# Softmax reciprocals through DRAM instead of through ACT and TensorE, in a hybrid RG-LRU and neighbourhood-attention layer

## The chip, the cores and the metric

One core of a Trainium2 chip runs the whole layer. The metric is the device time of one execution in microseconds; the number for a kernel is the median of its runs. Engines are called as in the profile: PE (TensorE), DVE (VectorE), ACT (ScalarE), POOL (GpSimd) and SP (SyncE, which here only issues DMAs). PEld is TensorE's loading of weights, which overlaps its matmuls.

## The reference

A sequence of 512 positions (a grid of 8 rows by 64 columns) with 1024 channels passes one layer: an RMS norm with a modulation, eight projections, a recurrent branch and a neighbourhood-attention branch, a gated merge and a final norm, all in float32. The change touches the attention branch (16 heads of 64 channels):

```
proj = h @ w_in;  xa, za, q, k, v, zb, ga, gb = split(proj)
for each grid row r:                       # its window is all 8 rows, 16 columns around the query's column
    s = einsum('bqhd,bwqkhd->bhqwk', q_r, k_win) * scale + bias
    p = softmax(s over the window)
    out_r = einsum('bhqwk,bwqkhd->bqhd', p, v_win)
y_b = out * silu(zb)
y_b = y_b @ w_pb
```

The kernel leaves the exponentials unnormalized. The product of p and v comes out with channels on the partitions and queries along the row. The sums of the softmax come out the other way: queries on the partitions, and one column for each block and head. Their reciprocals have to be brought from that layout to the other one, to every channel of the head, and are multiplied into silu(zb).

## The kernel before

The first part normalizes x and computes v (tiles hx), which goes to DRAM (vscr) and comes back in another layout (vt). Then comes a sequence of projections, each 24 matmuls of 128x128 by 512 columns into one PSUM bank (acc). Every float32 operand is split into a high part and a low part (whi and wlo, qh and ql, kh and kl, ybh and ybl), and three products replace one. ACT makes the high parts, DVE or POOL the low ones. The weights (wraw) come by DMA, 512 KB each, some projections ahead.

Attention runs over eight pairs of heads (`pr`). Each pair has three projections (q, k, z) and then `attention`: the scores (PSUM tiles sp, 24 matmuls, which read qh, ql, kh and kl), the bias and minimum on DVE (L721), exponentials on ACT with the sums into sm (L727), transposes of p (pt), the split pp, the product with vt (pv), and its three parts added up (vp, yt). While one pair is in its softmax, PE works on the projections of the next. The columns are cut into four blocks of 16 (`b`); a block's 128 queries lie on the partitions, so that sm is 128 x 8, two heads for each of four blocks. The last steps of a pair are

- rc (L775): the reciprocals of sm on DVE, 128 x 8
- rcx (L779): ACT repeats each of them 64 times, with a factor of 0.5, to 128 x 512
- rcb (L784): PE transposes the four 128x128 blocks into a PSUM bank (its tile is listed as mi)
- szr (L786): DVE multiplies sz, which is silu(zb) without its factor 0.5, by them
- yb (L788): DVE multiplies that by yt, then come ybh on ACT and ybl on DVE

ybh and ybl are read by the projections with w_pb, after all eight pairs.

The order of the instructions is made by a planner before the program is built (`Plan`). Every operation is given its engine, a cost, a rank and the tiles that it reads and writes; the planner places them one by one at the earliest estimated time. It hands out buffers of fixed pools (36 tiles of 2 KB a partition, 32 of 4 KB, 8 PSUM banks, with limits for each kind). `lock` keeps a DVE operation and one on POOL apart in that plan. The result is a fixed order on each engine, SP's queue included: an engine that waits for one operation holds back all that stands behind it. The bias (braw) is loaded by two DMAs a pair and made up on POOL (nb); vt is loaded by eight DMAs for every second pair.

Of the kernel before, what the change touches and what calls it, by code (L numbers as in the profile page):

```python
# [8 lines left out]
F32 = mybir.dt.float32  # L9
F32R = mybir.dt.float32r  # L10
AF = mybir.ActivationFunctionType
ALU = mybir.AluOpType

P = 128
# [54 lines left out]
class Plan:  # L69
# [18 lines left out]
    def op(self, eng, cost, fn, rank, r=(), w=(), rw=(), lock=False, after=(), spare=0, size=0, until=None, name=""):  # L88
        o = Op()
        o.alts = {eng: cost} if isinstance(eng, str) else dict(zip(eng, cost))  # L90
        o.fn, o.rank, o.lock, o.spare, o.size, o.name = fn, rank, lock, spare, size, name
        o.n, o.until = len(self.ops), until
        deps = set()
        for t in list(r) + list(rw):
            for f in t.family():
                deps.update(f.writers)
        for t in list(w) + list(rw):
            for f in t.family():
                deps.update(f.readers)
        for t in r:  # L100
            t.readers.append(o)
        for t in w:
            t.writers.append(o)
        for t in rw:
            for f in [t] + t.parts:
                f.writers, f.readers = [], []
            t.writers = [o]
        o.tiles = list(dict.fromkeys(t.base or t for t in list(w) + list(rw) + list(r)))
        for t in o.tiles:
            t.uses += 1  # L110
        o.data, o.succ, o.t = set(deps), [], 0.0
        deps.update(after)
        o.left = len(deps)
        for d in deps:
            d.succ.append(o)
        self.ops.append(o)
        return o
# [155 lines left out]
def act(n, ptr=0, acc=False):  # L273
    return 0.19 + 0.833e-3 * n + 0.093 * ptr + 0.19 * acc


def dve(n):
    return 0.153 + 1.043e-3 * n
# [15 lines left out]
def layer(ctx, tc, x, par, w_m, w_g, bc_gate, w_v, w_in, w_blk, rpb, amask, w_pa, w_pb, w_o, g_final, out):  # L294
    nc = tc.nc
# [4 lines left out]
    dp = ctx.enter_context(tc.tile_pool(name="dp", bufs=1, space=bass.MemoryType.DRAM))  # L300
    pl = Plan({"s": NS, "w": NW, "bank": 8}, LIMITS)
    op = pl.op
    cnt = [0]

    def nm(s):
        cnt[0] += 1
        return f"{s}_{cnt[0]}"

    def T(name, dt=F32):
        return pl.tile("s", lambda i: sb.tile([P, S], dt, tag=f"s{i}", name=nm(name)))  # L310
# [9 lines left out]
    def B(cls):  # L320
        return pl.tile(cls, lambda i: ps.tile([P, 512], F32, tag=f"b{i}", name=nm(cls)))

    def C(name, n, bufs=4):

        return pl.tile("c", lambda i: tp.tile([P, n], F32, tag=name, name=nm(name), bufs=bufs))
# [3 lines left out]
    def load(t, dst, src, rank, size, after=(), spare=0, r=(), name="load"):  # L329

        return op("SP", 0.45, lambda e: nc.sync.dma_start(dst(), src() if callable(src) else src), rank,
                  r=r, w=[t], after=after, spare=spare, size=size, name=name)
# [20 lines left out]
    def const(name, shape, dt=F32):  # L353
        return pl.fixed(cp.tile(shape, dt, name=name))

    ident, onesc, onesr = const("ident", [P, P]), const("onesc", [P, P]), const("onesr", [P, P], F32R)
# [11 lines left out]
       r=[par_sb, ident], w=[pp0])  # L368
# [54 lines left out]
    for t in range(NT):  # L423
        for h in range(2):
            a = xt[t, h] = T("x")
# [5 lines left out]
    for t in range(NT):  # L431
# [7 lines left out]
        if t % 2:  # L439
            rstd_ops(2, [qap[i], qdp[i]], lambda i=i: (qa.ap[:, 2 * i:2 * i + 2], qd.ap[:, 2 * i:2 * i + 2]), -16.8 + 2 * i, rx[i])  # L440
            for h in range(2):
                for u in (t - 1, t):
                    def scale(e, u=u, h=h, i=i):
# [6 lines left out]
                       lock=True)  # L450
# [165 lines left out]
    def proj(w, rh, rl, lo="DVE"):  # L616

        n = len(main)
        raw, hi, low = W("wraw"), W("whi", F32R), W("wlo", F32R)
        v = lambda t: (lambda: t.ap.rearrange("p (k c) -> p k c", k=KD))  # L620
        load(raw, whole(raw), w, n - 5, 524288, after=gate_of(n, 5), spare=1,
             name=f"w{n}")
        op("ACT", act(1024), cast(whole(hi), whole(raw)), n - 2.2, r=[raw], w=[hi], after=gate_of(n, 3), name=f"whi{n}")
        engs = (lo,) if isinstance(lo, str) else lo
        costs = [dve(1024) if e == "DVE" else pool_(1024) for e in engs]
        op(engs, costs, sub(whole(low), whole(raw), whole(hi)), n - 2.1, r=[raw, hi], w=[low], lock=True, name=f"wlo{n}")
        o = B("acc")
        for k in range(KD):
            def f(e, k=k):
                mm3(o.ap, v(hi)()[:, k, :], v(low)()[:, k, :], rh[k][1](), rl[k][1](), k == 0, k == KD - 1)  # L630
            first = op("PE", pe(512, 3), f, 1000 + n + 0.01 * k, r=[hi, low, rh[k][0], rl[k][0]], rw=[o], name=f"p{n}")
            if k == 0:
                main.append(first)
        return n, o


    H = (slice(0, 64), slice(64, 128))
# [3 lines left out]
    nat = lambda t: t.rearrange("p (b r c) -> p r b c", b=4, c=16)  # L641
    rbc = lambda t: t.rearrange("p (r b c) -> p r b c", b=4, c=16)
# [39 lines left out]
    def attention(pr, q, k, z, nbt, pos):  # L682
# [9 lines left out]
        sm, yt = C("sm", 8), T("yt")  # L692
# [4 lines left out]
        def scores(e_):  # L697
            for b, (kc0, w, _) in enumerate(BLOCKS):
                for i, (qt, kt) in enumerate(((qh, kh), (qh, kl), (ql, kh))):
                    for h in range(2):  # L700
                        kv = kt.ap.rearrange("p (r c) -> p r c", c=GW)[H[h], :, kc0:kc0 + w]
                        o = sps[b // 2][h].ap.rearrange("p (e f) -> p e f", e=2)[:, b % 2, :nkb[b]]
                        mm(o, qt.ap[H[h], b * P:(b + 1) * P], kv, i == 0, i == 2)
        op("PE", 1.45, scores, pos, r=[qh, ql, kh, kl], w=sps[0] + sps[1], name=f"qk{pr}")

        def half(b0):
            sp = sps[b0 // 2]
            spv = lambda h, e: sp[h].ap.rearrange("p (e f) -> p e f", e=2)[:, e, :]
            rk = pos + 0.1 * b0
            nks = nkb[b0:b0 + 2]  # L710
            pv = [B("pv"), B("pv")]
            for e in range(2):
                b, nk, w = b0 + e, nks[e], BLOCKS[b0 + e][1]
                nb = nbt[(1, 0, 0, 2)[b]]
                pt_, mn = T("p"), C("mn", 2, 16)
                hv = lambda t: t.ap.rearrange("p (h f) -> p h f", h=2)
                for h in range(2):
                    def f(e_, h=h, e=e, nk=nk, nb=nb, pt_=pt_, mn=mn):
# [49 lines left out]
        half(2)  # L768

        nz, oz = z  # L770
        sz, rc, rcb = T("sz"), C("rc", 8), B("mi")
        op("ACT", act(512), lambda e: nc.scalar.activation(sz.ap, oz.ap, AF.Tanh, scale=0.5), nz - 1.9, r=[oz], w=[sz], name="zt")
        op("DVE", dve(512), lambda e: nc.vector.scalar_tensor_tensor(sz.ap, sz.ap, 1.0, oz.ap, op0=ALU.add, op1=ALU.mult),
           nz - 1.9, r=[oz], rw=[sz], name="sz")
        op("DVE", 0.17, lambda e: nc.vector.reciprocal(rc.ap, sm.ap), pos - 0.3, r=[sm], w=[rc], name="rc")  # L775


        rx_ = T("rcx")
        op("ACT", act(512), lambda e: nc.scalar.activation(rx_.ap.rearrange("p (b c) -> p b c", b=8),  # L779
           rc.ap.unsqueeze(2).to_broadcast([P, 8, 64]), AF.Copy, scale=0.5), pos - 0.3, r=[rc], w=[rx_], name="rcx")  # L780

        def f(e_):
            for b in range(4):
                nc.tensor.transpose(rcb.ap[:, b * P:(b + 1) * P], rx_.ap[:, b * P:(b + 1) * P], ident.ap)  # L784
        op("PE", 0.47, f, pos - 0.3, r=[rx_, ident], w=[rcb], name="rcb")
        op("DVE", dve(512), lambda e: nc.vector.tensor_tensor(rbc(sz.ap), rbc(sz.ap), nat(rcb.ap), op=ALU.mult),  # L786
           pos - 0.3, r=[rcb], rw=[sz], name="szr")
        op("DVE", dve(512), lambda e: nc.vector.tensor_tensor(rbc(sz.ap), nat(yt.ap), rbc(sz.ap), op=ALU.mult), pos + 0.5, r=[yt],  # L788
           rw=[sz], lock=True, name="yb")
        ybh[pr], ybl[pr] = two("ybhl")  # L790
# [2 lines left out]
           name="ybl")  # L793
# [36 lines left out]
    for pr in range(8):  # L830
        n0 = len(main)
        nbt = bias(pr, n0, gate_of(n0, 2) if pr else [main[6]])
        if pr % 2 == 0:
            load_v(pr // 2, gate_of(n0, 2) if pr else [])
        q = proj(w_in[16 + pr], hhl, hll, LO_A if pr else "DVE")
        k = proj(w_in[24 + pr], hhl, hll, LO_A)
        z = proj(w_in[32 + pr], hhl, hll, LO_A)
        attention(pr, q, k, z, nbt, k[0] + 0.6)
# [199 lines left out]
    for k in range(KD):  # L1038
# [3 lines left out]
        for n in range(2):  # L1042
            v = lambda n=n, raw=raw: raw.ap[:, n * 512:(n + 1) * 512]
            op("DVE", dve(512), lambda e, n=n, v=v: nc.vector.tensor_tensor(v(), v(), gate[n].ap, op=ALU.mult), rank,
               r=[gate[n]], rw=[raw], lock=True, name="wog")
# [5 lines left out]
    for t in range(NT):  # L1051
        for h in range(2):
            a = xres[t, h] = T("xr")
# [51 lines left out]
    pos = [B("acc") for _ in range(NT)]  # L1105
# [8 lines left out]
    for t in range(NT):  # L1114
        for h in range(1 + (t == NT - 1)):
            w = 256 if t == NT - 1 else 512
# [87 lines left out]
```

## Time and profile before

| | before |
|---|---|
| median of 3 runs | 574.23 us (572.92 to 574.43) |
| profiled execution | 573.27 us, span 571.4 us |
| granted TensorE clock | 0.997 |
| instructions | 7735 |
| chain that ended last | PE 96%, DVE 2%, ACT 1% |
| DMA | 81.34 MB, mean 142 GB/s |

The span reaches from the first to the last instruction; the time of an execution includes a little around it. Times within the trace are given from the span's start. Attention runs from about 79 us (scores of pair 0) to about 262 us, one pair every 22.4 us. Rows of the timeline give the start, the length, the engine, the line, the operation, "output<-input" by tile names, and in brackets how long the engine sat idle and who ended it. Rows on a tile or line give the number of instructions and their shortest, median and longest duration in ns. Rows of windows give for each stretch the busy time and the number of instructions of PE, PEld, DVE, ACT and POOL, then the granted clock, the mean busy share of the 16 DMA engines and the GB/s. Matmuls overlap, so that their single durations add up to more than the time they take.

### The profile page before, as it was taken

The page shows a single profiled execution, that of the slowest core. Times are in us where ns is not written, and L with a number is a line of the kernel's source. Part 1 is how long each engine was busy: PE and PEld are TensorE (multiplying, and loading weights), DVE is VectorE, ACT ScalarE, POOL GpSimd, SP SyncE. Part 2 cuts the span into 40 slices and gives each one's busy share as a digit, 9 for nine tenths or more (in the row PEclk, how much of TensorE's full clock was granted, in tenths as well). Part 3 has the DMA queues.
Part 4 walks back from the last instruction along what each step waited for, and adds up shares of the span by engine and source line. Part 5 has one row for each costly group of instructions (what it writes and reads, how often), then busy time and mean ns, then how long its engine had stood idle before and what let it go on. Part 6 is the DMA issues. An engine that isn't in the chain of part 4 may idle for free.

```text
span 571.4 us, 7735 instructions
## 1 busy us (share of the span) xinstructions
PE 563.2 (99%) x2829; PEld 464.6 (81%) x2829; DVE 393.1 (69%) x693; ACT 336.6 (59%) x584; POOL 99.1 (17%) x84
## 2 busy tenths in 40 slices
PE   8999999999999999999999999999999999999995
PEld 6888888888888888887887787787788888888885
DVE  4997966575666657877389559749847996398323
ACT  5765537547556557478938876984894333234133
POOL 0005527374382570000000000000000000000220
PEclk9999999999999999999999999999999999999998
DMA  8993988544445322123232223123229813290002
GB/s 279 409 406 110 347 242 268 156 125 135 109 121 158 93 92 75 37 84 120 73 112 92 75 73 130 50 98 110 75 87 335 276 38 110 111 330 2 0 38 111
DMA packets 30815, 81.34 MB, mean 142 GB/s; under 512 B 3265, under 2 KB 6457, under 8 KB 30778
## 3 DMA queue, kind: packets, MB, share of 16 engines
q1 hardware_dynamic: 30633, 80.60, 42.1%
q8 instruction: 22, 0.36, 0.3%
q10 hardware_dynamic: 144, 0.26, 0.1%
q14 instruction: 16, 0.12, 0.1%
HBM read 74.56 MB, written 6.29 MB: 141 GB/s over the span
## 4 chain that ended last, share of the span: by engine, by line
PE 96%; DVE 2%; ACT 1%; issue 0%; POOL 0%; POOLq 0%; DVEq 0%; ACTq 0%
PE acc L342 77%; PE hx L342 7%; PE pv L342 3%; PE pt L736 2%; PE gt L342 2%; PE sp L342 2%; PE hx L386 1%; PE mi L784 1%; PE mi L457 1%; DVE wc L501 0%; PE hx L471 0%; ACT x L446 0%; DVE junk L436 0%; ACT xT L336 0%; ACT vh L336 0%
## 5 line engine op out<-in xcount | busy, mean ns | idle before, releaser
L342 PE MATMUL acc<-hhl,whi 128*128 128x512 f32 x784 | 246.1, 395 | 0.0
L342 PEld LDWEIGHTS acc<-hhl,whi 128*128 128x128 f32 x784 | 142.7, 188 | 29.0 <-issue 1.8
L342 PE MATMUL acc<-hhl,wlo 128*128 128x512 f32 x392 | 153.1, 390 | 0.0
L342 PEld LDWEIGHTS acc<-hhl,wlo 128*128 128x128 f32 x392 | 73.6, 188 | 16.0
L336 ACT CAST whi<-wraw 128x1024 fp32r<-128x1024 f32 x72 | 74.2, 1045 | 3.3 <-DMA wraw<-in_w_in_dram 2.5
L339 DVE TENSOR_TENSOR wlo<-wraw,whi 128x1024 fp32r<-128x1024 f32 x49 | 59.1, 1219 | 14.0 <-ACT whi L336 13.2
L339 POOL TENSOR_TENSOR wlo<-wraw,whi 128x1024 fp32r<-128x1024 f32 x23 | 56.0, 2439 | 68.4 <-ACT whi L336 47.0
L1075 POOL TENSOR_TENSOR yo<-yo,gfin 128x512 f32<-128x512 f32 x6 | 8.1, 1352 | 338.4 <-ACT xr L1072 338.3
L727 ACT ACTIVATE p<-p,mn 128x192 f32<-128x192 f32 (+1 forms) x64 | 30.4, 477 | 28.8 <-DVE mn L721 28.8
L662 POOL TENSOR_TENSOR nb<-msk,braw 128x192 f32<-128x192 f32 (+1 forms) x48 | 34.6, 756 | 55.4 <-DMA braw<-in_rpb_dram 55.4
L721 DVE CUSTOM_DVE_ANT_0 p<-sp,nb 128x192 f32<-128x192 f32 (+1 forms) x64 | 31.1, 615 | 16.7 <-PE sp L342 16.7
L342 PE MATMUL acc<-woh,mhl 128*128 128x512 f32 (+1 forms) x144 | 40.4, 365 | 0.0
L342 PE MATMUL acc<-yahl,whi 128*128 128x512 f32 x128 | 39.4, 389 | 0.0
L342 PE MATMUL acc<-ybhl,whi 128*128 128x512 f32 x128 | 39.4, 389 | 0.0
L952 DVE SCALAR_TENSOR_TENSOR gm<-gm,acc 128x512 f32<-128x512 f32 x16 | 11.0, 687 | 39.4 <-PE acc L342 39.4
L743 DVE TENSOR_TENSOR pp<-pt,pp 96x512 fp32r<-96x512 f32 (+1 forms) x32 | 22.0, 688 | 22.1 <-ACT pp L741 21.9
L342 PE MATMUL hx<-vh,hhl 128*128 128x512 f32 x112 | 35.3, 391 | 0.0
L342 PEld LDWEIGHTS acc<-woh,mhl 128*128 128x128 f32 x144 | 26.1, 189 | 4.4
L342 PEld LDWEIGHTS acc<-yahl,whi 128*128 128x128 f32 x128 | 24.0, 188 | 5.0
L342 PEld LDWEIGHTS acc<-ybhl,whi 128*128 128x128 f32 x128 | 24.0, 188 | 5.0
L342 PE MATMUL acc<-wol,mhl 128*128 128x512 f32 (+1 forms) x72 | 26.3, 365 | 0.0
L342 PE MATMUL acc<-yahl,wlo 128*128 128x512 f32 x64 | 24.9, 389 | 0.0
(186 smaller groups left out, 982.2 us busy)
## 6 DMA issues: line engine op xcount, KB each, us to landing
wraw<-in_w_in_dram SPq DMA_DIRECT2D x56, 512.0 KB
wc<-in_w_m_dram SPq DMA_DIRECT2D x16, 512.0 KB
vscr<-va SPq DMA_DIRECT2D x8, 512.0 KB
vt<-vscr SPq DMA_DIRECT2D x16, 256.0 KB
wraw<-in_w_pb_dram SPq DMA_DIRECT2D x8, 512.0 KB
wraw<-in_w_pa_dram SPq DMA_DIRECT2D x8, 512.0 KB
wr<-in_w_g_dram SPq DMA_DIRECT2D x16, 256.0 KB
wo<-in_w_o_dram SPq DMA_DIRECT2D x8, 512.0 KB
```

Source lines behind the costliest of these rows:

```text
L336: return lambda e: nc.scalar.copy(o(), i()) if e == "ACT" else nc.vector.tensor_copy(o(), i())
L339: return lambda e: ENGINE[e].tensor_tensor(o(), a(), b().bitcast(F32), op=ALU.subtract)
L342: nc.tensor.matmul(o, a, b, start=first, stop=last)
L386: op("PE", 0.9, lambda e, n=n, cb=cb: nc.tensor.matmul(cb.ap, onesc.ap[0:1, :], crow.ap[0:1, n * 512:(n + 1) * 512], start=True, stop=True ...
L457: op("PE", 0.3, lambda e: nc.tensor.matmul(wb.ap[:, :P], onesc.ap, onesc.ap, start=True, stop=True), 5000 + j, r=[onesc], w=[wb], until=un ...
L662: nc.gpsimd.tensor_tensor(o, mv, view, op=ALU.subtract)
L721: nc.vector.tensor_tensor_reduce(out=o, in0=v(spv(h, e)[:, :nk]), in1=v(hv(nb)[:, h, :nk]), scale=1.0, scalar=3e38, op0=ALU.add, op1=ALU.m ...
L727: nc.scalar.activation(hv(pt_)[:, h, :nk], hv(pt_)[:, h, :nk], AF.Exp, bias=mn.ap[:, h:h + 1], scale=-1.0, accum_out=sm.ap[:, 2 * b + h:2 ...
L736: nc.tensor.transpose(pv4()[:4 * w, h, j, :], hv(pt_)[:, h, j * 4 * w:(j + 1) * 4 * w], ident.ap)
L743: op("DVE", dve(512), lambda e_, w=w, ppv=ppv, pv4=pv4: nc.vector.tensor_tensor(ppv()[:4 * w, :, :, 1, :], pv4()[:4 * w], ppv()[:4 * w, :, ...
L952: op("DVE", dve(512), lambda e: nc.vector.scalar_tensor_tensor(t.ap, t.ap, 1.0, o.ap, op0=ALU.add, op1=ALU.mult), n - 1.9, r=[o], rw=[t], ...
L1075: op(("DVE", "POOL"), (dve(w), pool_(w)), lambda e: ENGINE[e].tensor_tensor(y(), y(), gfin[n].ap[:, gs], op=ALU.mult), rank + 0.1, r=[gfin ...
```

## The change

The reciprocals are written to a small DRAM tensor (rscr, 8 x 128, one for each pair) with their axes swapped, and read back by two DMAs, one for each head, that repeat the head's four rows of 128 queries on its 64 partitions. The factor 0.5 is put in by doubling the sums before the reciprocal. The repeat on ACT, the four transposes on PE and the PSUM bank go away; the product szr reads SBUF instead of PSUM.

```
-        sz, rc, rcb = T("sz"), C("rc", 8), B("mi")
+        sz, rc, rcx = T("sz"), C("rc", 8), T("rcx")
...
-        op("DVE", 0.17, lambda e: nc.vector.reciprocal(rc.ap, sm.ap), pos - 0.3, r=[sm], w=[rc], name="rc")
+        op("DVE", 0.34, lambda e: (nc.vector.tensor_scalar(rc.ap, sm.ap, 2.0, None, op0=ALU.mult), nc.vector.reciprocal(rc.ap, rc.ap)),
+           pos - 0.3, r=[sm], w=[rc], name="rc")
-        rx_ = T("rcx")
-        op("ACT", act(512), lambda e: nc.scalar.activation(rx_.ap.rearrange("p (b c) -> p b c", b=8),
-           rc.ap.unsqueeze(2).to_broadcast([P, 8, 64]), AF.Copy, scale=0.5), pos - 0.3, r=[rc], w=[rx_], name="rcx")
-        def f(e_):
-            for b in range(4):
-                nc.tensor.transpose(rcb.ap[:, b * P:(b + 1) * P], rx_.ap[:, b * P:(b + 1) * P], ident.ap)
-        op("PE", 0.47, f, pos - 0.3, r=[rx_, ident], w=[rcb], name="rcb")
-        op("DVE", dve(512), lambda e: nc.vector.tensor_tensor(rbc(sz.ap), rbc(sz.ap), nat(rcb.ap), op=ALU.mult),
-           pos - 0.3, r=[rcb], rw=[sz], name="szr")
+        scr = pl.fixed(dp.tile([8, P], F32, name=f"rscr{pr}"))
+        op("SP", 0.5, lambda e: nc.sync.dma_start(scr.ap.rearrange("a q -> q a"), rc.ap), pos - 3, r=[rc], w=[scr], size=4096,
+           name="rcs")
+        for h in range(2):
+            src = bass.AP(scr.ap.tensor, scr.ap.offset + h * P, [[0, 64], [2 * P, 4], [1, P]])
+            load(rcx, lambda h=h: rcx.ap[H[h], :].rearrange("p (b q) -> p b q", b=4), src, pos - 3, 131072, r=[scr], name="rcl")
+        op("DVE", dve(512), lambda e: nc.vector.tensor_tensor(rbc(sz.ap), rbc(sz.ap), nat(rcx.ap), op=ALU.mult),
+           pos - 0.3, r=[rcx], rw=[sz], lock=True, name="szr")
```

The planner sets the order anew. On DVE, pair 0 before, from the reciprocals to the first bias step of pair 1 (numbers tell buffers apart, ISA is the bias step):

```order
L775 RECIPROCAL rc_976<-sm_889 128x8
L339 TENSOR_TENSOR ql_1003<-acc_898,qh_996 128x512
...
L743 TENSOR_TENSOR pp_1015<-pt_981,pp_1015 96x4x128
L786 TENSOR_TENSOR sz_908<-sz_908,mi_1032 128x512
...
L764 TENSOR_TENSOR yt_1025<-pv_1041,vp_1065 64x256
L788 TENSOR_TENSOR sz_908<-yt_1025,sz_908 128x512
L690 SCALAR_TENSOR_TENSOR kl_1100<-acc_990,kh_1094 128x512
L339 TENSOR_TENSOR ybhl_1103<-sz_908,ybhl_1103 128x512
L721 ISA p_1148,mn_1149<-sp_1114,nb_879 128x8x24
```

The same place after the change:

```order
L775 TENSOR_SCALAR rc_984<-sm_897 128x8
L775 RECIPROCAL rc_984<-rc_984 128x8
L339 TENSOR_TENSOR ql_1013<-acc_906,qh_1006 128x512
...
L743 TENSOR_TENSOR pp_1017<-pt_991,pp_1017 96x4x128
L785 TENSOR_TENSOR sz_916<-sz_916,rcx_1031 128x512
...
L764 TENSOR_TENSOR yt_1033<-pv_1046,vp_1071 64x256
L690 SCALAR_TENSOR_TENSOR kl_1109<-acc_1000,kh_1096 128x512
L787 TENSOR_TENSOR sz_916<-yt_1033,sz_916 128x512
L721 ISA p_1153,mn_1154<-sp_1117,nb_887 128x8x24
```

The product with the reciprocals keeps its place; kl comes ahead of yb, and ybl moves into the bias steps of the next pair. On SP's queue, around the same time before (braw is the bias, vt the values, wraw the weights):

```order
L331 DMA wraw_902<-in_w_in_dram 128x1024
L331 DMA braw_994<-in_rpb_dram 128x1x256 x2
L331 DMA vt_1005<-vscr_86 96x1x512
L331 DMA vt_1009<-vscr_86 96x1x512
L331 DMA vt_1017<-vscr_86 128x1x512
...
L331 DMA wraw_1169<-in_w_in_dram 128x1024
L331 DMA braw_1260<-in_rpb_dram 128x1x256 x2
L331 DMA wraw_1271<-in_w_in_dram 128x1024
L331 DMA wraw_1336<-in_w_in_dram 128x1024
```

And after the change, through pair 0 and pair 1:

```order
L331 DMA wraw_910<-in_w_in_dram 128x1024
L780 DMA rscr_88<-rc_984 128x8x1
L331 DMA braw_1004<-in_rpb_dram 128x1x256 x2
L331 DMA vt_1015<-vscr_86 96x1x512
L331 DMA vt_1019<-vscr_86 96x1x512
L331 DMA rcx_1031<-rscr_88 64x4x128 x2
L331 DMA vt_1042<-vscr_86 128x1x512
...
L780 DMA rscr_89<-rc_1248 128x8x1
L331 DMA braw_1268<-in_rpb_dram 128x1x256 x2
L331 DMA wraw_1279<-in_w_in_dram 128x1024
L331 DMA rcx_1293<-rscr_89 64x4x128 x2
```

The store to rscr stands ahead of the pair's braw, and two vt (even pairs) or one wraw (odd pairs) stand between it and the loads of rcx. From pair 6 on there is no braw left; one wraw stands between.

## The prediction

> **What bounds the kernel now.** I read the page's busy times first, then the chain of work that ended last around the first attention pair, then that pair on VectorE, and last the DMA queue.
>
> ```profile
> PE 563.2 (99%) x2829; PEld 464.6 (81%) x2829; DVE 393.1 (69%) x693; ACT 336.6 (59%) x584; POOL 99.1 (17%) x84
> ```
>
> TensorE works 99% of the span; no other engine is over 69%. So the time is TensorE's own work plus whatever makes it wait. The chain between 85 and 106 us (start, length, what), a stretch that holds the softmax and the second pair's scores:
>
> ```profile
> by line: PE acc L342 76.5%; PE pv L342 9.1%; PE sp L342 7.5%; PE pt L736 6.3%; PE mi L784 2.1%
> ...
> 94.14 0.44 PE mi L784 x4
> 94.58 0.47 PE pv L342 x4
> ...
> 96.22 5.46 PE acc L342 x24
> 101.68 1.57 PE sp L342 x24
> ```
>
> Every piece is TensorE, with no gap. The four transposes of the reciprocals (mi, L784) hold it for 0.44 us. The scores of the next pair (sp) are the next piece that needs something attention-bound from VectorE: kl, the low half of k.
>
> **What is removed.** All transposes, and the ACT work that feeds them:
>
> ```profile
> L784 PE MATMUL mi<-ident,rcx x32: 272/273/273, 94.0 to 250.6; 128*128 128x128 f32 x32
> ```
>
> That row would be wrong to use for the cost: 273 ns each is pipelined time. The chain's 0.44 us for four is what TensorE loses, and eight pairs make 8 x 0.44 = 3.5 us, all on the path since TensorE has no slack. The other removals:
>
> ```profile
> L779 ACT ACTIVATE rcx<-rc x8: 630/632/633, 92.0 to 249.1; 128x512 f32<-128x512 f32 x8
> ```
>
> ACT gets 8 x 0.63 us back. I cost that at nothing: ACT is busy 59% and does not appear in the quoted chain. The freed PSUM bank is also nothing, since no piece above waits for a bank.
>
> **What is added, on VectorE.** Its timeline through pair 0 (start, length, instruction, in brackets the idle time before and who ended it), and one instruction of the added kind:
>
> ```profile
> 4.99 0.17 DVE L375 TENSOR_SCALAR mods<-prm 128x8 f32<-128x8 f32 x1
> ```
>
> ```profile
> 89.67 0.19 DVE L775 RECIPROCAL rc<-sm 128x8 f32<-128x8 f32 x1
> ...
> 94.61 0.69 DVE L786 TENSOR_TENSOR sz<-sz,mi 128x512 f32<-128x512 f32 x1
> 96.41 0.88 DVE L761 TENSOR_TENSOR vp<-pv,vp 64x256 f32<-64x256 f32 x2 [1.11 <-ACT vp L758]
> 97.32 0.88 DVE L764 TENSOR_TENSOR yt<-pv,vp 64x256 f32<-64x256 f32 x2
> 98.24 1.15 DVE L788 TENSOR_TENSOR sz<-yt,sz 128x512 f32<-128x512 f32 x1
> 99.41 0.69 DVE L690 SCALAR_TENSOR_TENSOR kl<-acc,kh 128x512 fp32r<-128x512 f32 x1
> ```
>
> ```profile
> 101.81 0.27 PE L342 MATMUL sp<-kl,qh 64*128 64x192 f32 x2
> ```
>
> The extra doubling takes 0.2 us with its gap, so the reciprocals are ready at 89.67 + 0.2 + 0.19 = 90.06. The product with them (sz<-sz,mi; the change calls its source rcx) keeps its place: behind it in VectorE's fixed order stand two vp, two yt, and kl, which now comes ahead of yb (sz<-yt,sz). If the product can start at X, about 0.62 later vp starts, and kl ends 98.24 + 0.69 - 96.41 = 2.52 after that: X + 3.14. The scores would stand at 101.68 - 0.44 = 101.24 and read kl 0.2 us in; allowing a tenth for the signal and some of those 0.2, I want kl by about 101.1. The product now reads SBUF alone, as yb does, and yb took 1.15 us at 98.24 where kl took 0.69; 0.46 us more behind each wait would be 2.8 us in six pairs, which I leave to the range. So X may be as late as 97.95: **the way through DRAM has 7.9 us**, and what it takes beyond that TensorE waits, in full.
>
> **What is added, on the DMA queue.** One store of 128x8 numbers with its axes swapped (1024 pieces of 4 bytes, 64 for each of 16 DMA engines), then two loads of 64x4 rows of 512 bytes (512 rows, 32 an engine). All go through SP's queue. No transfer of 4-byte pieces is in the trace. Nearest are the first load, 120 rows of 512 bytes (the line of GB/s has 40 slices of 0 to 3.2 us, 0.08 each), and the last store:
>
> ```profile
> 0.74 0.46 SPq L331 DMA_DIRECT2D par_sb<-in_par_dram  x1
> ```
>
> ```profile
> GB/s 2 0 0 0 0 0 0 0 0 0 0 0 0 0 0 0 0 0 0 0 0 0 70 90 154 173 109 0 0 0 0 51 90 224 167 154 282 333 384 384
> ```
>
> ```profile
> 567.51 0.33 SPq L1098 DMA_DIRECT2D out_dram<-yo  x1
> ```
>
> ```profile
> SPq L1200 <- DMA out_dram<-yo: 2.1, 1, 2.1
> ```
>
> ```profile
> 567.00:567.50 0.50, 0.00 (x0) 0.00 (x0) 0.48 (x1) 0.45 (x1) 0.00 (x0) 0.99 0.00 0
> 567.50:568.00 0.50, 0.00 (x0) 0.00 (x0) 0.00 (x0) 0.00 (x0) 0.00 (x0) 0.50 0.00 0
> 568.00:568.50 0.50, 0.00 (x0) 0.00 (x0) 0.00 (x0) 0.00 (x0) 0.00 (x0) 0.50 0.27 102
> ...
> 569.50:570.00 0.50, 0.00 (x0) 0.00 (x0) 0.00 (x0) 0.00 (x0) 0.00 (x0) 0.50 0.47 168
> ```
>
> In the windows the last three columns are granted clock, DMA share and GB/s. The store was issued at 567.51 and moved from about 568.4 (0.9 us later) to 569.7; the wait of 2.1 us from the end of issue ended at 569.9, 0.2 after the data. The first load began to move 1.0 us after its issue and had most of its rows through in five slices, 0.40 us for about eight an engine: 50 ns a row. I take 50 ns for a 4-byte piece too: 64 x 0.05 = 3.2 us. The ends: nothing beyond the start and landing (4 KB in all), and 128 ns, the time of a 2 KB row of vt below, which makes 8.2 us.
>
> What stands between store and loads counts, because the engines take SP's queue in order. By the new order that is two braw and two vt in pairs 0, 2 and 4, two braw and a 512 KB weight tile in pairs 1, 3 and 5:
>
> ```profile
> 80.94 2.51 SPq L331 DMA_DIRECT2D braw<-in_rpb_dram  x2
> 83.49 10.10 SPq L331 DMA_DIRECT2D vt<-vscr  x8
> 93.65 2.34 SPq L331 DMA_DIRECT2D wraw<-in_w_in_dram  x3
> ```
>
> ```profile
> 145.32 1.32 SPq L331 DMA_DIRECT2D braw<-in_rpb_dram  x2
> ```
>
> ```profile
> 146.00:146.50 0.50, 0.50 (x5) 0.15 (x3) 0.00 (x0) 0.00 (x0) 0.50 (x1) 1.00 0.00 0
> 146.50:147.00 0.50, 0.50 (x9) 0.50 (x10) 0.00 (x0) 0.00 (x0) 0.50 (x1) 1.00 0.29 16
> ...
> 149.00:149.50 0.50, 0.50 (x4) 0.41 (x3) 0.50 (x5) 0.20 (x2) 0.00 (x0) 1.00 0.43 129
> 149.50:150.00 0.50, 0.50 (x3) 0.38 (x3) 0.50 (x5) 0.00 (x0) 0.00 (x0) 1.00 1.08 410
> ```
>
> ```profile
> 97.00:99.00 2.00, 2.00 (x10) 1.68 (x9) 1.90 (x4) 1.45 (x2) 2.00 (x5) 1.00 0.85 255
> ```
>
> Two braw (256 KB) alone on the queue occupy it from 146.5 to 149.5, 3.0 us, before the weights take over at 410 GB/s. Two vt of 192 KB at the 255 GB/s of the loaded queue take 1.5 us, a weight tile 1.3 to 2.0. A 2 KB row at 255/16 GB/s is the 128 ns used above.
>
> From the ready reciprocals: start 0.9, store 3.2 (4.1), braw 3.0 (7.1), vt or weights 1.5 (8.6), the loads, landing 0.2. The loads are 1.6 us by the first load's 50 ns, 3.0 by braw, which moves the same 256 KB in two DMAs; I take the middle, 2.3. That is **11.1 us against 7.9: a wait of 3.2 us**. With the queue empty in between, SP sees the store at 4.3, its second load issues 0.66 later (half of braw's 1.32), moves 1.2 after that (145.32 to 146.5) for at least half of 2.3, and lands: 7.5. So even without neighbours nothing is to spare.
>
> It happens where the product stands close behind the reciprocals and kl behind it: pairs 0 to 5, six times. In pair 6 it does not:
>
> ```profile
> 224.22 0.19 DVE L775 RECIPROCAL rc<-sm 128x8 f32<-128x8 f32 x1
> ```
>
> ```profile
> 236.99 1.57 PE sp L342 x24
> ```
>
> There the queue holds one weight tile and no braw between: 11.1 - 3.0 = 8.1 us from 224.6 gives X = 232.7, kl at 235.8, and the scores at 236.99 lose nothing. Behind pair 7 no scores follow.
>
> On SP braw, vt and weights now stand behind the wait for rc, and vt and weights behind the landed store too. I cost that at nothing, because they come early:
>
> ```profile
> 111.76 1.03 ACT L336 CAST whi<-wraw 128x1024 fp32r<-128x1024 f32 x1
> 112.87 2.41 POOL L339 TENSOR_TENSOR wlo<-wraw,whi 128x1024 fp32r<-128x1024 f32 x1 [9.73 <-ACT whi L336]
> ```
>
> The weights issued at 93.65 are first cast at 111.76. Behind the loads and six vt they issue at about 101 and land by 107. The braw behind rc lands near 97.3; if that delays GpSimd's bias work by a microsecond, GpSimd's 9.7 us idle before 112.87 absorbs it.
>
> One rule of the Trainium skill speaks against the change. DMA: Bandwidth & Descriptors, Rules for kernel authors, says that a strided last dimension becomes one descriptor per element. No run here shows it yet. Without that rule 4 KB would move in almost nothing, the wait would be zero and the change would gain its 3.5 us.
>
> **The sum.** 6 x 3.2 - 3.5 = +15.7 us. The profiled execution took 573.27 us (span 571.4), 0.96 below the median of 574.23: 589.0 against that execution, 590 against the median.
>
> **Rivals.**
> - Faster: the round trip fits into 7.9 us, by a store under 10 ns a piece (0.6 us) with the queue as above, or by neighbours that overlap it. For it: 4 KB are few bytes, and 7.5 us was the sum on an empty queue. Against: two braw always stand between. It gives 574.23 - 3.5 = 570.7. It turns at a wait of 3.5/6 = 0.58 us.
> - No change: a wait of 0.3 to 0.87 us, which takes back the gain within the 0.3% (1.7 us) that a measurement of this kernel can tell: 572.5 to 576. The store would have to take 0.3 to 0.9 us, 5 to 14 ns a piece; the 50 ns row speaks against it. The Trainium skill, DMA: Bandwidth & Descriptors, section Bandwidth (Measured), gives about 10.5 ns a packet as the floor of a small transfer; by that, as an estimate, the store is 0.7 us, the wait 0.7, the sum +0.7. The first load's rows took five times that.
> - Much slower: pieces at 128 ns, a wait of 8.2, +46 us, 620. Written pieces may cost more than read rows; the trace can't say.
> - A clock that falls in the waits. The last matmul of the kernel:
>
> ```profile
> 564.52 0.28 PE L342 MATMUL acc<-woh,mhl 128*128 128x256 f32 x1
> ```
>
>   It ends at 564.8, and the granted clock is 0.50 from 567.5, after 2.7 us of idle time. A wait of 3.2 us may reach that; if as long again ran at half speed, 1.35 us would be lost each time, 8 in all: 598.
>
> **Chances.** The wait of 1 to 6 us, with or without a clock loss (576 to 606): 0.55, where 590 stands. Faster 0.20. No change 0.10. Over 606: 0.15. The range of 570 to 612 leaves out some 0.05 below and 0.12 above; the likeliest case's own is 576 to 606. Faster by over 0.3%: 0.2; within: 0.1; slower: 0.7.
>
> **What would show it.** The product on VectorE idle before it on a DMA into rcx, about 3 us in pairs 0 to 5 (right), or not at all (rival one). Idle time of TensorE ahead of sp of the same size. The L784 pieces gone from the chain, and the stretch from 96.22 on earlier by 0.44 a pair. The DMA windows after each rc tell the store's time apart from braw's. I am wrong if the 4-byte pieces go at a few ns, or if braw does not hold up what stands behind it.

## The result, and the profile after

| | before | after |
|---|---|---|
| median of 6 runs each | 573.73 us (572.89 to 574.43) | 664.36 us (659.67 to 665.57) |
| profiled execution, span | 573.27 us, 571.4 us | 659.67 us, 657.9 us |
| granted TensorE clock | 0.997 | 0.937 |

The change makes the kernel slower, by a ratio of 1.157 (95% interval 1.155 to 1.159), 90.6 us in the medians. The forecast was 590 us in a range of 570 to 612. The profiled execution is the quickest of the six, 4.7 us below the median; the accounts below are made against its span.

From the page of after: busy time, the chain that ended last by engine and line, and TensorE's granted clock in 40 slices.

```profile
PE 577.1 (88%) x2797; PEld 474.7 (72%) x2797; DVE 398.2 (61%) x701; ACT 332.2 (50%) x576; POOL 93.2 (14%) x84
...
PEclk9999996977879796979897999999999999999999
...
PE 67%; DMA 20%; DVE 7%; ACT 2%; SPq 2%; issue 1%; DVEq 0%; ACTq 0%
```

TensorE was busy 99% of the span before and is busy 88% now, and a fifth of the chain is DMA, which was absent. Nor does it run at full clock any more: the low digits lie in the stretch of attention, slices 7 to 22 (16.4 us each). The span grew by 86.5 us. TensorE's idle time grew from 571.4 - 563.2 = 8.2 to 657.9 - 577.1 = 80.8 us, by 72.6, and its busy time by 13.9 although the transposes went away.

The waits of after (who waited, on whom: us in total, times, longest):

```profile
DVE sz L785 <- DMA rcx<-rscr: 89.9, 8, 14.0
PE sp L342 <- DVE kl L690: 66.5, 7, 11.7
PE gt L342 <- ACT xh L336: 2.9, 1, 2.9
SPq L331 <- DMA rscr<-rc: 63.4, 8, 10.0
```

The first two rows are the chain that the prediction described: the product on DVE waits for the DMA, and TensorE's scores wait for kl, which stands behind the product. They give 66.5 of the 72.6 us. The waits come in seven pairs, not six, and average 9.5 us, not 3.2. Behind the eighth pair, where no scores follow, the gates of the recurrent branch (gt) waited 2.9 us.

Pair 0 step by step, first in the chain (start, length, what), then on DVE, TensorE and POOL:

```profile
89.95 9.20 DMA rscr<-rc
...
99.17 4.50 SPq L331
...
103.71 2.96 DMA rcx<-rscr
...
106.76 2.69 DVE sz L785
...
111.17 0.70 DVE kl L690
...
111.92 2.66 PE sp L342 x15
```

```profile
89.72 0.20 DVE L775 RECIPROCAL rc<-rc 128x8 f32<-128x8 f32 x1
...
106.76 2.69 DVE L785 TENSOR_TENSOR sz<-sz,rcx 128x512 f32<-128x512 f32 x1 [12.22 <-DMA rcx<-rscr]
```

```profile
101.00 0.36 PE L342 MATMUL sp<-kh,qh 64*128 64x192 f32 x2
111.92 0.53 PE L342 MATMUL sp<-kl,qh 64*128 64x192 f32 x2 [10.56 <-DVE kl L690]
```

```profile
106.56 2.34 POOL L339 TENSOR_TENSOR wlo<-wraw,whi 128x1024 fp32r<-128x1024 f32 x1
```

The reciprocals are ready at 89.92 and the scores stand at 101.00, where the prediction had them at 101.24. The store to rscr takes until 99.15. SP, which waited for it, issues the first load at 99.17 and needs 4.50 us for that, where the median issue of such a load takes 0.62. By 99.15 at most 0.33 of the 0.66 MB of bias and values issued behind the store had moved (36 GB/s from 90 us on), so the load probably waits for them; no view shows it. The second load lands at 106.66. The product then takes 2.69 us instead of 0.69; the POOL operation beside it lasts to 108.90, the product to 109.45. TensorE stands still for 10.56 us and then runs its scores in 2.66 us; they took 1.57 before.

### The profile page after: what moved, and what is told of

Same layout as the page of the kernel before. It is cut to its first block, busy times and chain, and to the rows that moved or that the text cites. A ratio compares the mean times of both kernels' runs of the same rounds, so it can differ in the third digit from the quotient of the medians.

```text
span 657.9 us, 7704 instructions
## 1 busy us (share of the span) xinstructions
PE 577.1 (88%) x2797; PEld 474.7 (72%) x2797; DVE 398.2 (61%) x701; ACT 332.2 (50%) x576; POOL 93.2 (14%) x84
## 4 chain that ended last, share of the span: by engine, by line
PE 67%; DMA 20%; DVE 7%; ACT 2%; SPq 2%; issue 1%; DVEq 0%; ACTq 0%
PE acc L342 54%; DMA rscr<-rc 13%; PE hx L342 6%; DMA rcx<-rscr 6%; PE sp L342 3%; DMA x<-in_x_dram 2%; PE gt L342 2%; SPq L331 2%; DVE sz L785 2%; PE pt L736 1%; DVE yt L764 1%; DVE vp L761 1%; ACT pp L741 1%; DVE kl L690 1%; DVE pp L743 1%
## 5 line engine op out<-in xcount | busy, mean ns | idle before, releaser
L342 PE MATMUL acc<-hhl,whi 128*128 128x512 f32 x784 | 252.6, 404 | 0.0
L342 PEld LDWEIGHTS acc<-hhl,whi 128*128 128x128 f32 x784 | 146.7, 193 | 31.2 <-issue 3.6
L342 PE MATMUL acc<-hhl,wlo 128*128 128x512 f32 x392 | 155.3, 396 | 0.0
L342 PEld LDWEIGHTS acc<-hhl,wlo 128*128 128x128 f32 x392 | 75.7, 193 | 16.7
L342 PE MATMUL sp<-kl,qh 64*128 64x192 f32 (+1 forms) x64 | 13.5, 420 | 66.5 <-DVE kl L690 66.5
L785 DVE TENSOR_TENSOR sz<-sz,rcx 128x512 f32<-128x512 f32 x8 | 12.3, 1534 | 89.9 <-DMA rcx<-rscr 89.9
L342 PEld LDWEIGHTS sp<-kl,qh 64*128 64x128 f32 x64 | 9.7, 301 | 67.7 <-DVE kl L690 67.7
L336 ACT CAST ybhl<-sz 128x512 fp32r<-128x512 f32 x8 | 4.9, 619 | 96.8 <-DVE sz L787 96.8
L662 POOL TENSOR_TENSOR nb<-msk,braw 128x192 f32<-128x192 f32 (+1 forms) x48 | 28.8, 629 | 99.8 <-DMA braw<-in_rpb_dram 94.2
```

The source lines that it names most:

```text
L336: return lambda e: nc.scalar.copy(o(), i()) if e == "ACT" else nc.vector.tensor_copy(o(), i())
L342: nc.tensor.matmul(o, a, b, start=first, stop=last)
L662: nc.gpsimd.tensor_tensor(o, mv, view, op=ALU.subtract)
```

## The experiments

Two things could make the round trip long, the store's 4-byte pieces and its neighbours in the queue; and one thing decides what that costs, the product's place ahead of kl. Each was changed by itself, then together. The planner sets the order anew in every run; where it moved the product in a way that was not meant, the text says so. Time of the kernel before beside them: 573.55 to 573.73 us.

### e1: the same 4 KB store in 128 pieces of 32 bytes

```
-  nc.sync.dma_start(scr.ap.rearrange("a q -> q a"), rc.ap)
+  nc.sync.dma_start(bass.AP(scr.ap.tensor, scr.ap.offset, [[8, P], [1, 8]]), rc.ap)
```

> The kernel after, but the store writes its 4 KB row by row (128 pieces of 32 bytes, 8 a DMA engine, instead of 1024 of 4 bytes, 64 an engine); the loads keep their shape and so read the reciprocals of other queries. Theory pieces (the store costs about 0.15 us a piece and engine): the store lands about 1.1 + 8 x 0.15 = 2.3 us after its issue instead of 11.0, the wait ahead of the product falls by 8.7 us a pair to about 1 us or less in pairs 5 to 7 and 1 to 4 us in the others; time 570 to 590 us. Theory bytes or receipt (a write to DRAM that is read back costs its 10 us whatever the pieces): the store still lands after 9 us or more, time over 640 us.

596.67 us, ratio 1.043 (1.036 to 1.049): the store landed even sooner than the theory of the pieces said, but the time lies above its 570 to 590. The rows of e1 on the store and on the waits (the first row, here and in the runs below, tells of the last pair's store alone):

```profile
DMA to landing us min/median/max: 1.4/1.4/1.4
```

```profile
DVE sz L785 <- DMA rcx<-rscr: 32.5, 7, 5.6
PE sp L342 <- DVE kl L690: 15.3, 7, 3.3
```

The same row of after, from issue to landing of the store:

```profile
DMA to landing us min/median/max: 11.0/11.0/11.0
```

Nothing but the size of the pieces differs, and it is worth 68 us. But 23 us of loss are left with a store that takes 1.4 us. What remains is the way of the loads (chain of e1, then its DMA in two windows; the last three columns are granted clock, DMA share and GB/s):

```profile
95.27 5.96 DMA rcx<-rscr
```

```profile
91.00:99.00 8.00, 8.00 (x44) 6.77 (x43) 3.12 (x7) 4.98 (x9) 6.75 (x6) 1.00 0.58 137
99.00:101.25 2.25, 2.25 (x12) 1.86 (x11) 0.00 (x0) 0.67 (x2) 2.25 (x4) 1.00 1.03 244
```

### e2: the same store in 512 pieces of 8 bytes

```
+  nc.sync.dma_start(bass.AP(scr.ap.tensor, scr.ap.offset, [[2, P], [2 * P, 4], [1, 2]]),
+                    rc.ap.rearrange("p (b h) -> p b h", h=2))
```

> The kernel after, but the store writes 512 pieces of 8 bytes (32 an engine); the loads read wrong places again. Theory pieces: landing about 1.1 + 32 x 0.155 = 6 us after issue, half the way between the kernel after and 128 pieces; time 605 to 630 us. Theory bytes or receipt: landing stays near 11 us, time 655 to 668 us.

606.28 us, ratio 1.057 (1.053 to 1.061). The rows of e2:

```profile
DMA to landing us min/median/max: 4.9/4.9/4.9
```

```profile
PE sp L342 <- DVE kl L690: 24.0, 7, 5.4
```

With 8, 32 and 64 pieces for each of 16 DMA engines the store of the last pair lands after 1.4, 4.9 and 11.0 us: (4.9 - 1.4) / 24 = 0.15 and (11.0 - 4.9) / 32 = 0.19 us more for each piece that an engine has. Over all eight pairs SP goes on to the loads 4.3 to 5.0 us after the store's issue in e2, and 9.2 to 11.1 us after it in the change. The bytes are the same, so the landing goes by the pieces. That is a slope of the landing, not a time for which an engine is busy with a piece (see the last section).

The step from e1 to e2 costs 10 us, that from e2 to the change 58. In pair 0 of e1 SP issues bias and values for 3.4 us before it comes to the loads, so a store that lands sooner than that gains nothing there.

### e3: after's store, but the product planned behind kl

The planner is told that store and loads take longer. It then puts the product behind kl and the first bias steps of the next pair.

```
-  ... w=[scr], size=4096, name="rcs")
+  ... w=[scr], size=3200000, name="rcs")
-  load(rcx, ..., pos - 3, 131072, r=[scr], name="rcl")
+  load(rcx, ..., pos - 3, 600000, r=[scr], name="rcl")
```

> The kernel after with the same DMAs, but the planner is told that the store takes 8.3 us more and the loads 1.2 us more each; so it puts the product with the reciprocals behind kl and the bias steps of the next pair on VectorE. Theory place (the time is lost only because kl and the scores stand behind a product that waits): no wait ahead of the scores, the granted clock back at 0.997, 569 to 576 us. Rival hold (SP's queue, which waits 9 to 10 us a pair for the store, delays weights, values and bias): 580 to 620 us, with waits on braw, vt or wraw.

583.82 us, ratio 1.019 (1.015 to 1.023). The waits of e3:

```profile
PE pv L342 <- DVE pp L743: 6.4, 4, 2.5
PE sp L342 <- DVE kl L690: 0.4, 1, 0.4
SPq L331 <- DMA rscr<-rc: 45.0, 5, 10.2
```

The 66.5 us before the scores are down to 0.4, with the same slow store: the place of the product carried that loss. But it is not free: the time lies above the 569 to 576 of the theory of the place and within the 580 to 620 of its rival, 14 us above the 570 of e6 below. The product still idles DVE, now ahead of pp, and 6.4 us of TensorE's waits stand behind that; SP also still holds the queue until the store has landed. How the rest shares out is not shown.

### e4 and e7: the DMAs alone

Both keep the old path through ACT and TensorE. e4 adds the store and both loads, into a tile that nothing reads; e7 adds the store alone.

```
   op("PE", 0.47, f, pos - 0.3, r=[rx_, ident], w=[rcb], name="rcb")
+  scr = pl.fixed(dp.tile([8, P], F32, name=f"rscr{pr}"))
+  op("SP", 0.5, lambda e: nc.sync.dma_start(scr.ap.rearrange("a q -> q a"), rc.ap), ...)
+  # e4 alone: two loads of rscr into rcx2 = T("rcx2")
```

> The kernel before with its ACT and TensorE path, plus the store and the two loads of the change, whose result nothing reads. Theory place: nothing on VectorE or TensorE waits for them, 572 to 578 us. Rival hold (the store's 1024 pieces and SP's wait for them cost time by themselves): 585 us or more.

> The old path with the store of 1024 pieces beside it that nothing reads, and no loads. e4, with the two loads as well, took 581.58 us, 8.0 over before. Theory (the store alone occupies SP's queue for its 11 us and delays what stands behind it): the bias behind it lands late all the same, 578 to 583 us. Rival (the landed store's wait on SP and the buffers of the loads did it): SP then never stops for the store's landing, so values and weights are issued as early as before, and the time is 573.5 to 576 us.

e4: 581.58 us, ratio 1.015 (1.013 to 1.018). e7: 577.37 us, ratio 1.006 (1.005 to 1.008). The waits of e4, then of e7:

```profile
ACT sz L772 <- DMA rcx<-rscr: 11.0, 3, 5.2
PE pt L736 <- ACT p L727: 2.8, 2, 1.8
```

```profile
PE mi L784 <- ACT rcx L779: 0.7, 1, 0.7
```

Both lie between the two expectations. The store costs 3.6 us even where nobody needs it. Its trace, of a run 1.7 us below the median, has only 1.5 us of TensorE's waits in attention (the longest is shown), so where the 3.6 us come from stays open. The loads and SP's wait for the store add 4.2. Part of these are of the experiment's own making: the unread tile's buffer goes to the next pair's sz, and ACT waits 11.0 us for the loads before it may overwrite it. So "the DMAs alone cost 3.6 to 8 us" is shown, and how they share it is not.

### e5: e1's store without neighbours

Bias and values are planned one step earlier, so that they stand ahead of the store and not between it and its loads. In pairs 1 to 5 the planner also moved the product, from ahead of the last vp and yt to behind them, still ahead of kl; in pair 0 it kept its place.

```
-  nbt = bias(pr, n0, gate_of(n0, 2) if pr else [main[6]])
+  nbt = bias(pr, n0, gate_of(n0, 3) if pr else [main[6]])
-  load_v(pr // 2, gate_of(n0, 2) if pr else [])
+  load_v(pr // 2, gate_of(n0, 3) if pr else [])
```

> The 128-piece store of e1 (wrong queries' reciprocals), and the planner may load bias and values one projection earlier, which puts two braw and all vt ahead of the store on SP's queue; one 512 KB weight tile stays between store and loads, and the product keeps its place. In e1 the second load lands 6.0 us after its issue in pair 0, and seven waits of TensorE for kl sum to 15.3 us. Theory neighbours (the engines take the queue in order, so braw's 3.0 and vt's 1.5 us stand ahead): the second load lands about 4 us after its issue, TensorE's waits for kl sum to under 5 us, time 574 to 583 us. Rival loads (512 rows that all read the same 4 KB are slow by themselves): landing stays near 6 us, waits over 12 us, time over 588 us.

579.21 us, ratio 1.010 (1.008 to 1.011): 17.5 us less than e1. The waits and the chain of e5 in pair 0:

```profile
PE sp L342 <- DVE kl L690: 2.7, 6, 1.5
```

```profile
94.64 5.81 DMA rscr<-rc
...
101.19 3.03 DMA rcx<-rscr
```

In pair 0 the loads now take 3.03 us where e1's took 5.96. In exchange the store takes 5.81 us with SP's issue, although its pieces are as few as e1's, probably because values are still under way ahead of it; from its issue to the product's start it is 9.67 us, against 10.15 in e1. In pairs 1 to 5 SP goes on to the loads 1.4 us after the store's issue, and the product, in its later place, waits for nothing. So the loads are quicker without neighbours, as forecast, and in pair 0 moving the neighbours shifts most of it ahead. How the 17.5 us share out between the neighbours and the later place is not shown.

### e6: nothing in the path's place

The repeat on ACT, the transposes and any DMA are left out; sz is multiplied by one column of rc, so the softmax isn't normalized rightly.

> The kernel before without the way of the reciprocals: no repeat on ACT, no four transposes, no DRAM; the product is a multiplication of sz with one column of the reciprocals, so the normalization is wrong. It prices what the change removes. Theory chain (0.44 us of TensorE a pair, nothing else): 3.5 us less than before, 570.2 us (ratio 0.994). Rival: the slots were filled by waits anyway, under 1 us less.

570.10 us, ratio 0.993 (0.992 to 0.995), with this busy time:

```profile
PE 560.4 (99%) x2797; PEld 462.7 (81%) x2797; DVE 399.0 (70%) x693; ACT 332.5 (58%) x576; POOL 98.1 (17%) x84
```

The removal is worth 3.5 us in the medians (3.2 to 4.6 by the interval), as the prediction read from the chain (8 x 0.44); TensorE's busy time is less by 2.8 us. 570.1 is what a replacement could reach if all of it were hidden.

### f1, f2 and f3: the transpose on DVE, and a store of long pieces

DVE transposes rc in 32x32 blocks, so that 8 partitions of a block hold 32 queries each in a row; four stores write 8 rows of 128 bytes (32 pieces a pair instead of 1024). f1 also takes e3's cost for the loads; f3 is f1 without it, so that the product stands ahead of kl again; f2 is f1 with e5's earlier bias and values.

```
+        nc.vector.memset(rc.ap, 1.0)                       # rc, rct: 128 x 32
+        nc.vector.tensor_scalar(rc.ap[:, :8], sm.ap, 2.0, None, op0=ALU.mult)
+        nc.vector.reciprocal(rc.ap[:, :8], rc.ap[:, :8])
+        nc.vector.transpose(rct.ap, rc.ap)
...
+        for g in range(4):
+            op("SP", 0.4, lambda e, g=g: nc.sync.dma_start(scr.ap[:, 32 * g:32 * g + 32], rct.ap[32 * g:32 * g + 8, :]), ...)
```

> The change with the swap of axes made by VectorE (a transpose of 32x32 blocks into a 128x32 tile) and four stores of 8 rows of 128 bytes each, and with the loads' cost in the planner raised from 0.34 to 1.56 us each. Theory: stores land within 2 us of the last issue, the product stands behind kl in most pairs, 571 to 580 us. Rival hold (SP's wait for rc and the four issues delay weights and bias): over 580 us.

> f1 with bias and values loaded one projection earlier, so that they stand ahead of the stores. Theory place with neighbours gone: no wait of TensorE for VectorE, the removed 3.5 us are kept: 569 to 573 us, faster than before. Rival hold: 575 us or more, with waits behind braw, vt or wraw.

> The blocks of f1, with the planner's cost of the loads left as in the change, so that the product stands ahead of the last yt and of kl again. In f1 the loads were issued by SP at 97.02 to 98.33 behind two braw and three vt; landing 3 to 5 us later they give the product's start at 101.3 to 103.3. Then come the product (0.69), yt (0.44) and kl (0.69), so that kl ends 1.8 later, at 103.1 to 105.1, where f1's scores read it at 102.47. Theory (the place of the product matters as well as the store): TensorE waits 0.6 to 2.6 us, most likely 1.5, in pairs 0 to 5; 570.1 + 6 x 1.5 = 579 us, range 573 to 587, with PE sp waiting for DVE kl. Rival (the store was all): no wait of PE sp for kl above 0.3 us, 570 to 572 us.

| | time | ratio to before |
|---|---|---|
| f1 | 570.14 us | 0.994 (0.992 to 0.995) |
| f2 | 576.33 us | 1.004 (1.003 to 1.006) |
| f3 | 596.97 us | 1.040 (1.038 to 1.043) |

f1 beats both kernels, a little below its expected 571 to 580 us, and equals e6, so it keeps all of the 3.5 us. Its busy time, its one wait of TensorE (that of the kernel's start, which before has too), and DVE in pair 0:

```profile
PE 560.6 (99%) x2797; PEld 462.9 (81%) x2797; DVE 396.0 (70%) x717; ACT 331.2 (58%) x576; POOL 94.1 (17%) x84
```

```profile
PE mi L457 <- POOL onesc L360: 1.5, 1, 1.5
```

```profile
91.76 0.21 DVE L779 STREAM_TRANSPOSE rct<-rc 128x32 f32<-128x32 f32 x1
...
99.75 0.69 DVE L690 SCALAR_TENSOR_TENSOR kl<-acc,kh 128x512 fp32r<-128x512 f32 x1 [0.18 <-ACT kh L689]
...
103.76 0.69 DVE L790 TENSOR_TENSOR sz<-sz,rcx 128x512 f32<-128x512 f32 x1
```

kl is made before the product, and the product, 4 us later, has no bracket: it waits for nothing.

f3 executes the same instructions with the product ahead of kl. Its busy time, the wait, and the chain and windows of pair 1:

```profile
PE 570.5 (96%) x2797; PEld 469.8 (79%) x2797; DVE 400.2 (67%) x717; ACT 331.8 (56%) x576; POOL 93.3 (16%) x84
```

```profile
PE sp L342 <- DVE kl L690: 17.5, 6, 3.5
```

```profile
121.81 6.71 DMA rcx<-rscr
```

```profile
129.00:132.00 3.00, 0.00 (x0) 0.00 (x0) 2.94 (x3) 0.00 (x0) 1.43 (x1) 1.00 0.15 59
132.00:133.50 1.50, 1.29 (x21) 1.29 (x22) 1.04 (x3) 0.62 (x1) 0.00 (x0) 0.97 0.00 0
134.00:136.00 2.00, 2.00 (x5) 1.61 (x6) 2.00 (x9) 0.75 (x4) 0.00 (x0) 0.50 0.00 0
```

TensorE waits for kl in six pairs, as the theory (the place matters too) said, but the time missed its range: 597 against 573 to 587. The waits were 2.9 us and not 1.5, and something was added that the expectation did not have. f3's span is 27.4 us longer than f1's (595.8 against 568.4): 17.5 us are the waits, and 570.5 - 560.6 = 9.9 us are the same 2797 matmuls taking longer. The windows show why: after 3.5 us without work TensorE runs at half clock from about 133.4 us on. The clock fell after five of the six waits.

f2 missed its expectation. TensorE waits once, at the start of attention (rows of TensorE and ACT):

```profile
89.27 1.10 PE L736 MATMUL pt<-ident,p 128*96 128x128 f32 x4 [5.97 <-ACT p L727]
```

```profile
87.72 1.04 ACT L336 CAST whi<-wraw 128x1024 fp32r<-128x1024 f32 x1 [11.70 <-DMA wraw<-in_w_in_dram]
```

On SP's queue the earlier bias stands ahead of a weight tile, ACT waits 11.70 us for a weight tile, and the exponentials stand behind the cast. So loads that go earlier can push others later.

Four of these kernels, and the change itself, make one table (us):

| product | 1024 pieces of 4 bytes | few pieces |
|---|---|---|
| ahead of kl | 664.4 (the change) | 597.0 (f3) |
| behind kl | 583.8 (e3) | 570.1 (f1) |

Either mend alone leaves a loss. The late place takes off 81 us with the slow store and 27 with the quick one: with the product behind kl the round trip is largely covered. The upper row is not a change of the store alone, since f3's product stands behind two vp and one yt where that of the change stands ahead of them. And e5, with its product ahead of kl but behind vp and yt in five pairs, comes to 579.2 us.

## Why the prediction was right in direction and wrong in size

**Right: what is removed.** 3.5 us, shown by e6 and f1.

**Right: the mechanism, its place and its budget.** The waits stand where the prediction put them, and e3 takes them away by moving the product. kl would have been in time up to 101.1; the scores stood at 101.00.

**The step that failed: 50 ns for a written 4-byte piece.** It was taken from rows of 512 bytes that were read, and made the store 3.2 us long. The store of pair 0 was done 9.2 us after the reciprocals, not 4.1, and those of the other pairs 9.8 to 11.1 us after their issue; e1 and e2 show 150 to 190 ns a piece of an engine in the last pair. The upper end of the range, 128 ns for a 2 KB row of vt, puts the store's end at 9.1 us: nearly that of pair 0, and too early for the others. Both ends were prices of reading long rows, and no row of that trace priced a small written piece, so that one end came near was luck. The "much slower" rival (620 us) went by it and had a wait of 8.2 us where 9.5 were measured. It lacked the clock, the longer product and the seventh wait, and deserved more than the 0.15 that it had.

The rule cited there, from the Trainium skill (DMA: Bandwidth & Descriptors, Rules for kernel authors), that a strided last dimension becomes a descriptor for each element, agrees with the trace, which has 1040 packets of under 512 bytes between 326 and 328 us, behind the issue of the last pair's store (shown in the last section). The 10.5 ns a packet of the Trainium skill (the same page, Bandwidth (Measured)), which the "no change" rival used, is stated for loads issued by GpSimd, and for the time in which the DMA engines are busy. The records of the pieces agree with it in size: 1023 lie in one microsecond, 16 ns for each of the 64 of an engine. But the landing, for which SP waits, came 9 us later, and the rival had no term for that.

**About right in pair 0, in part by luck: neighbours and loads.** Forecast 3.0 + 1.5 + 2.3 + 0.2 = 7.0 us behind the store; from 99.15 to the product's start at 106.76 it was 7.6. But 4.5 of these are SP's issue of the first load, which the sum did not have. Not right was that what SP has issued is passed in strict order. In e1, by the windows shown, 1.10 MB had moved by 99 us and 1.65 MB by 101.25, when they landed; all that stood up to and with them was 0.92 MB, and nothing older was under way at 91. So transfers issued behind them ran beside them, and a quick store alone did not bring the gain.

**Mis-sized: the product, taken at its old length.** The prediction left 0.46 us to the range. It took 692 to 2691 ns in after:

```profile
L785 DVE TENSOR_TENSOR sz<-sz,rcx x8: 692/1782/2691, 106.8 to 340.9; 128x512 f32<-128x512 f32 x8
```

In pair 0 that is 2.0 us on the path behind the wait, and over the eight pairs 6.8 us more than at 0.69 each. In pairs 0 to 5 the product began while a POOL operation that also reads SBUF was running, as at 106.56, and each time ended 0.55 us after that operation (so did the six of f3); in pairs 6 and 7, with none beside it, it took 0.69. Behind pair 5's product POOL's next operation took 2.80 us instead of 2.34. So the two did not run at once: the later one stood until the earlier was done. The Trainium skill (GPSIMD Engine Reference, Key points) says that GpSimd shares its SBUF interfaces with VectorE and that they contend where a VectorE instruction has two SBUF inputs. That fits. Before, the product at 94.61 took one operand from PSUM and 0.69 us, with the same POOL work beside it (POOL's timeline of before):

```profile
94.09 2.40 POOL L339 TENSOR_TENSOR wlo<-wraw,whi 128x1024 fp32r<-128x1024 f32 x1 [1.14 <-ACT whi L336]
```

So in pair 0 the wait of 3.2 us became 10.56: 5.1 more by the store, 0.6 by the neighbours and loads, 2.0 by the product, less 0.3 of allowances.

**Six waits, seven in fact.** Pair 6 was left out because 8.1 us fitted its gap. With the store at 10.9 they don't. The chain's rows of pair 6, where no bias stands between:

```profile
296.09 10.86 DMA rscr<-rc
...
307.94 3.16 DMA rcx<-rscr
```

The product starts at 311.19, 15.1 us after the reciprocals. The exception hung on the same mis-sized term.

**The clock: a rival that came true beside the forecast.** It had been given 8 us, on top of waits of 3.2. f1 executes the same 2797 matmuls at a granted clock of 0.999 in 560.6 us of busy time, after in 577.1: 16.5 us for the eight times that the clock fell (behind the seven waits and that of the gates), 2.1 each. f3 shows 9.9 for its five, 2.0 each. No run kept the waits and the clock apart, so the split rests on TensorE's busy time.

**Costed at nothing: SP's hold.** No run prices it by itself. e7, where SP never waits for the store, costs 3.6 us; e4, where it does, 8.0, part of it by the buffer of the unread tile; of e3's 14 us 6.4 are waits behind the late product. So the DMAs did cost something beyond the late product, where the prediction had nothing; how much of that is the hold stays open.

The measured terms are 66.5 (waits before the scores) + 6.1 (other idle time, 2.9 of it the gates) + 16.5 (clock) - 2.6 (TensorE's busy time in f1 against before, 563.2 - 560.6) = 86.5 us, the growth of the span. They add up by construction, since idle and busy time make up the span.

## What to carry to other kernels

A DMA that swaps axes by its access pattern costs by pieces: count them, and do the swap on an engine (here 0.2 us on DVE) so that what is written is rows. A wait is priced by what stands behind it in the fixed order of its engine: where a result isn't needed at once, put its consumer behind the work that others wait for, before trying to shorten its way. And where no row of the trace is like an added operation, a bound from an unlike row is no bound.

## What the runs showed of the hardware that was not expected

- The time of a store of small pieces does not lie in the records of its pieces. That of the last pair of after was issued at 326.06 and landed at 337.10. All its pieces are recorded before 328 (first row, 326 to 328 us); from there to 337 the queue moved a few weight rows at 28 GB/s (second row), with the DMA engines recorded as 0.70 busy. What lasts behind the pieces grows with their number (e1, e2), but what it is, and whether it is paid by each DMA engine or by the store as a whole, no run shows.

```profile
DMA packets 1040, 0.00 MB, mean 2 GB/s; under 512 B 1040, under 2 KB 1040, under 8 KB 1040
DMA packets 58, 0.25 MB, mean 28 GB/s; under 512 B 0, under 2 KB 0, under 8 KB 57
```

- The clock falls with a delay that varies: 2.3 us after TensorE stopped at 101.36 in pair 0, 4.6 us after 136.52 in pair 1, 2.7 us in the kernel's tail before. In f3 it fell at 133.4 us, 1.2 us after work had begun again at 132.2, so that a wait of 3.5 us was charged later; there a wait of 2.4 us was enough for a fall, and one of 2.0 was not. Windows of after: the falls in pairs 0 and 1, the idle time of TensorE in pair 1, and the stretch at half clock:

```profile
103.50:103.75 0.25, 0.00 (x0) 0.00 (x0) 0.00 (x0) 0.00 (x0) 0.00 (x0) 0.72 0.59 213
141.00:141.25 0.25, 0.00 (x0) 0.00 (x0) 0.00 (x0) 0.00 (x0) 0.25 (x1) 0.82 0.90 215
136.50:141.00 4.50, 0.02 (x2) 0.00 (x0) 0.00 (x0) 0.00 (x0) 1.50 (x3) 1.00 0.71 192
141.50:152.00 10.50, 3.78 (x25) 3.42 (x26) 7.13 (x16) 1.60 (x5) 3.70 (x4) 0.50 0.27 84
```

The eight falls of after, at 103.6, 141.2, 175.3, 212.8, 247.0, 281.1, 311.8 and 349.4 us, lie 11, 10, 11, 10, 10, 9 and 11 times 3.41 us apart. So the falls lie on a grid, and the delay depends on where a wait lies in it. The Trainium skill (TensorE: Matmul & The Clock Gate, Part 1) has a free-running window of about 3.4 us and half rate after an idle one. The grid and the half rate (0.50) agree; but the window need not be idle throughout, since that of the first fall, from 100.2 us on, had work until 101.36.

- The product on DVE, with both operands in SBUF, did not run beside a POOL operation that reads SBUF: it took up to 2.7 us instead of 0.69, and ended 0.55 us after POOL's.
